# Stick-breaking attention with TensorE's order written out, the next pair's projections woven in, and products moved to GpSimd

## The chip, the cores and the metric

One core of a Trainium2 chip runs the whole program. The metric is device time in microseconds: 2575.24 us before (median of three runs, 2574.47 to 2579.44). Engines are named as the profile names them: PE is TensorE (PEld its weight loads), DVE is VectorE, ACT is ScalarE, POOL is GpSimd, SP issues the DMAs.

## The reference

A trunk of two layers over 1,024 rows of 1,024 features. Each layer is a token mixer and a SwiGLU. Layer 0 mixes with sliding-window attention (16 query heads, 2 key heads, window 128, softmax with sinks), layer 1 with stick-breaking attention (16 heads of 64). What the change touches most is the latter:

```
z = einsum('bqhd,bshd->bhqs', qb, k) * scale          # qb: 128 queries of one block
log_beta = log_sigmoid(z)
log_one_minus = where(strict, log_sigmoid(-z), 0.0)   # strict: key index < query index
rc = cumsum(log_one_minus, axis=3, reverse=True)
after = pad(rc[..., 1:], one column of zeros at the end)
a = where(strict, exp(log_beta + after), 0.0)
o = einsum('bhqs,bshd->bqhd', a, v)
```

In words: the weight of a key is sigmoid(z) times the product of sigmoid(-z) over all later keys before the query.

## The kernel before, in words

Every f32 matrix product runs on rounded halves: a value is split into a high part (an ACT cast to fp32r) and a low part (value minus high, a DVE or POOL subtraction), and three products stand for one (`mm3`, L100: high x high, high x low, low x high).

**The stages** on the trace's clock: norms and conditioning to about 120 us; sliding-window attention to about 345 us (`stage1` to `stage3`, L473 to L556); its output projection with the next norm (`out_proj`, L626) to about 480 us; SwiGLU to about 1165 us (`gates`, `down`); stick-breaking attention to about 1780 us (L965 to L1141); then out_proj and SwiGLU of layer 1 with the same functions.

**Stick-breaking** goes by pairs of heads, p = 0 to 7. `proj_pair(p)` (L1020) makes Q, K and the low part of K (`kl`) for two heads, and V: 3 weights x 2 halves of the rows x 8 blocks of the features x 3 products = 144 matmuls of 512 columns into banks `psd`. Each head's Q holds its high part in 64 partitions and its low part in the other 64, so that K and `kl` are needed in both halves of the partitions: L1037 to L1044 make the doubles with four more ACT casts per half.

Then 8 steps per pair, one for each head `par` and each block `c` of 256 queries. `attn_a` (L1067) takes two tiles of 128 queries, i = 2c and 2c+1, with L = 128(i+1) keys: score matmuls into `psz` (two, and a mask), two sigmoids on ACT (L1084 `nb` with the sign turned, L1085 `bb`), a reversed running product of `nb` on DVE in place (L1089, the scan; its two inputs `nb` and `ones` both lie in SBUF), and the product `bb` x `nb` on DVE (L1091, both inputs in SBUF too). `attn_v` (L1095) takes the finished tiles 256 keys at a time: four transposes into `pst` (L1103), the high part `ah` on ACT (L1106), the low part `al` on DVE (L1107; it reads `pst` in PSUM and `ah` in SBUF), four matmuls with V into `psa`. V's two halves of 64 columns give the high and low results in two halves of the partitions: `tm` (L1114) copies one half, `ob` (L1115) adds, and a DMA stores 64 rows. The steps come in the order c = 0, 3, 1, 2 for each head, `attn_v` one step behind `attn_a` (`lag`, L1122). `proj_pair(p+1)` is emitted behind the eight steps of pair p.

**What sets the order:** the program is emitted as above, and a scheduler of the framework orders each engine's instructions by emission, readiness and its own costs; each engine then runs its list strictly in order. So the projections of the next pair do stand between the steps of this one, where the scheduler put them. Pair 7 has no projections beside it; it loads and splits the output weights instead (`load_o`, L353, eight times: a DVE product L356, an ACT cast L298, a DVE split L299).

**Output projection** (`out_proj`, `block`, L632): a block of 128 rows loads the stored attention result, ACT casts it, POOL subtracts (L636, in `split_into` L299), PE multiplies. Sliding-window attention stores its result as stick-breaking does (L552 to L556: `tm`, `ob` with one buffer, 64 rows).

Of the kernel before, what the change touches and what calls it, by code (L numbers as in the profile page):

```python
# [18 lines left out]
P = 128  # L19
# [45 lines left out]
def build(tc, x_in, c_in, pos_in, ada_w, ada_b, n1g, n2g, wqkv_a, qn_a, kn_a, sinks, wo_a,  # L65
# [30 lines left out]

    def mm(o, l, r, start, stop, more=False):
        nc.tensor.matmul(o, l, r, start=start, stop=stop, skip_group_check=more)  # L98
# [6 lines left out]
    def tr(o, i, n=P):  # L105
        nc.tensor.transpose(o, i, ident[:n, :n])  # L106
# [280 lines left out]
    odA = [dr.tile([HD, 16, P], F32, name=f"odA{b}") for b in range(NB)]  # L387
# [41 lines left out]
    def keys_values(b):  # L429
# [20 lines left out]
        for j in range(4):  # L450
            nc.tensor.transpose(pt[:, j * P : (j + 1) * P], kdf[:, j], identr)
# [37 lines left out]
    def stage2(g, b, qs, r):  # L489
        QT = wk.tile([P, 8, P], F32R, tag="QT", name=nm("QT"), bufs=2)  # L490
        qsf = qs.rearrange("p h e d -> p h (e d)")
        for j in range(2):
            pt = bank("t", F32R)
            for h in range(4):
                nc.tensor.transpose(pt[:, h * P : (h + 1) * P], qsf[:, 4 * j + h], identr)
            nc.scalar.copy(QT[:, 4 * j : 4 * j + 4], pt.rearrange("p (h t) -> p h t", t=P))
# [34 lines left out]
    def stage3(g, b, sm):  # L531
        for j in range(2):
# [93 lines left out]
    def out_proj(p, W, od, x_src, l, gi, first):  # L626
# [338 lines left out]
    def nt_tile(shape, dt):  # L965
        return nbp.tile(shape, dt, tag="nt", name=nm("nt"), bufs=3)

    def load_b(p, j):
        raw = ad.tile([P, KT, P], F32, tag="ad", name=nm("wr"), bufs=2)
        nc.sync.dma_start(raw, wB[:, j * D + p * P : j * D + (p + 1) * P].rearrange("(k p) n -> p k n", p=P))  # L970
        t = wqp.tile([P, 2, KT, P], F32R, tag="whl", name=nm("whl"), bufs=4)
        return split_into(t[:, 0], t[:, 1], raw, scale=0.125 if j == 0 else None)
# [33 lines left out]
    odB = [dr.tile([HD, 16, 256], F32, name=f"odB{c}") for c in range(4)]  # L1006

    def proj_t(p, j):
        wh, wl = w0[j] if p == 0 else load_b(p, j)
        for half in range(2):  # L1010
            th, tl = HB[half]
            if p == 0 and half == 0 and j in first_b:
                pb = first_b[j]
            else:
                pb = bank("d")
                for k in range(KT):
                    mm3(pb, wh[:, k], wl[:, k], th[:, k], tl[:, k], k == 0, k == KT - 1)
            yield half, pb

    def proj_pair(p):  # L1020
# [4 lines left out]
        V = wb.tile([P, NB, 2, P], F32R, tag="V", name=nm("V"), bufs=1)  # L1025
        A, B = slice(0, HD), slice(HD, P)

        def q_(half, pb):
            s = slice(half * 512, half * 512 + 512)
            nc.scalar.copy(Q[0][A, s], pb[A])  # L1030
            nc.scalar.copy(Q[1][B, s], pb[B])
            sub(Q[0][B, s], pb[A], Q[0][A, s])
            sub(Q[1][A, s], pb[B], Q[1][B, s])

        def k_(half, pb):
            s = slice(half * 512, half * 512 + 512)
            nc.scalar.copy(K[0][A, s], pb[A])  # L1037
            nc.scalar.copy(K[1][B, s], pb[B])
            nc.scalar.copy(K[0][B, s], pb[A])
            nc.scalar.copy(K[1][A, s], pb[B])  # L1040
            sub(kl[0][A, s], pb[A], K[0][A, s])
            sub(kl[1][B, s], pb[B], K[1][B, s])
            nc.scalar.copy(kl[0][B, s], kl[0][A, s].bitcast(F32))
            nc.scalar.copy(kl[1][A, s], kl[1][B, s].bitcast(F32))  # L1044

        if p == 0:
            q_(0, first_b[0])
            k_(0, first_b[1])
        for half, pb in proj_t(p, 0):
            if p or half:  # L1050
                q_(half, pb)
        for half, pb in proj_t(p, 1):
            if p or half:
                k_(half, pb)
        for half, pb in proj_t(p, 2):
            vt = nt_tile([P, 512], F32)
            nc.scalar.copy(vt, pb)
            pt = bank("t")
            for b in range(4):
                tr(pt[:, b * P : (b + 1) * P], vt[:, b * P : (b + 1) * P])  # L1060
            v4 = pt.rearrange("p (b u d) -> p b u d", u=2, d=HD)
            o = V[:, half * 4 : half * 4 + 4]
            nc.scalar.copy(o[:, :, :, 0:HD], v4)
            sub(o[:, :, :, HD:P], v4, o[:, :, :, 0:HD])
        return Q, K, kl, V

    def attn_a(p, par, c, Q, K, kl, V):  # L1067
        bs = []
        for i in (2 * c, 2 * c + 1):
            L = P * (i + 1)  # L1070
            n = max(256, L if L <= 512 else L // 2)
            nb = wb.tile([P, S], F32, tag="nb", name=nm("nb"), bufs=2)
            bb = wb.tile([P, S], F32, tag="bb", name=nm("bb"), bufs=4)
            tq = slice(i * P, i * P + P)
            for s0 in range(0, L, n):
# [46 lines left out]
    def step(p, par, c, cur, lag):  # L1122
        pend.append(attn_a(p, par, c, *cur))
        while len(pend) > lag:
            attn_v(*pend.pop(0))
# [55 lines left out]
```

## Time and profile before

| | us |
|---|---|
| median of three runs | 2575.24 |
| the profiled execution, its own time | 2575.87 |
| its span, first to last instruction | 2574.1 |
| PE busy in the span | 2392.6 (93%) |
| DVE busy | 1679.6 (65%) |
| ACT busy | 1069.7 (42%) |
| POOL busy | 478.4 (19%) |

The mean granted clock of PE is 0.968 of full. Busy shares are means over stages with different limits, and a busy PE is not a PE at its peak, since a matmul's end is modelled and overlaps the next one: a matmul of 512 columns is shown with 390 ns and more, and follows the one before by 227 ns where PE is not held up. So a stage is judged by what its matmuls would take at their undisturbed spacing, against the time that it takes.

### The profile page before, as it was taken

How to read it: one execution, taken by the hardware profiler on the slowest of the kernel's cores; microseconds unless marked ns; L12 is line 12 of the kernel's file. 1: busy time of each engine (PE TensorE's matmuls, PEld its weight loads, DVE VectorE, ACT ScalarE, POOL GpSimd, SP SyncE). 2: the span in 40 equal slices, each digit the busy share in tenths (PEclk: the TensorE clock that was granted, in tenths of full speed). 3: DMA queues.
4: the chain of work that ended last, by engine and by line, in shares of the span. 5: the costliest groups of instructions: out<-in, count | busy, mean ns of one | idle time of the engine just before them, and what ended most of it. 6: DMA issues, size and time to landing. Idle time of an engine off the chain costs nothing.

```text
span 2574.1 us, 31259 instructions
## 1 busy us (share of the span) xinstructions
PE 2392.6 (93%) x11404; PEld 1937.7 (75%) x11404; DVE 1679.6 (65%) x2509; ACT 1069.7 (42%) x2077; POOL 478.4 (19%) x545
## 2 busy tenths in 40 slices
PE   6898788899999999999999999997989999999999
PEld 5776667678787878887777777776768888887887
DVE  7689854765767667436888777777365544557553
ACT  4487633423232232115666666664343333333110
POOL 2344533122232300001000000002213223220000
PEclk9799889899999999999999999998989999999999
DMA  8113266233535364202101111013412222226311
GB/s 280 49 42 93 82 173 201 66 110 125 175 122 180 106 229 143 71 25 83 40 26 28 28 33 32 24 41 96 140 53 91 91 66 90 92 80 236 104 50 66
DMA packets 159033, 248.59 MB, mean 97 GB/s; under 512 B 10256, under 2 KB 109728, under 8 KB 158880
## 3 DMA queue, kind: packets, MB, share of 16 engines
q1 hardware_dynamic: 158256, 246.46, 30.2%
q8 instruction: 90, 1.47, 0.2%
q14 instruction: 63, 0.52, 0.1%
q10 hardware_dynamic: 624, 0.14, 0.0%
HBM read 198.33 MB, written 48.23 MB: 96 GB/s over the span
## 4 chain that ended last, share of the span: by engine, by line
PE 67%; DVE 15%; ACT 5%; DMA 5%; issue 4%; POOL 3%; SPq 0%; ACTq 0%; DVEq 0%; POOLq 0%
PE psz L98 23%; PE psd L98 20%; PE pst L98 17%; PE psa L98 6%; DVE nb L1089 4%; DMA ada<-in_ada_w_dram 3%; DVE bb L1091 2%; DVE al L109 1%; DVE acc L258 1%; ACT sm L525 1%; PE pst L106 1%; POOL rg L299 1%; ACT ah L1106 1%; DVE sl L623 1%; DVE ob L1115 1%
## 5 line engine op out<-in xcount | busy, mean ns | idle before, releaser
L622 ACT CAST sh<-rg 128x512 fp32r<-128x512 f32 x308 | 191.5, 622 | 563.6 <-PE psz L98 252.4
L623 DVE TENSOR_TENSOR sl<-rg,sh 128x512 fp32r<-128x512 f32 x308 | 236.5, 768 | 79.5 <-ACT sh L622 79.5
L98 PE MATMUL psd<-hth,whl 128*128 128x512 f32 x768 | 255.8, 399 | 0.6 <-DVE QK L109 0.6
L298 ACT CAST dh<-raw 128x1024 fp32r<-128x1024 f32 x88 | 87.8, 1049 | 279.3 <-PE psa L98 176.1
L1089 DVE TENSOR_TENSOR_SCAN nb<-nb,ones 128x128 f32<-128x128 f32 (+7 forms) x128 | 170.4, 1343 | 29.7 <-ACT nb L1084 28.7
L98 PE MATMUL psd<-htl,whl 128*128 128x512 f32 x384 | 156.5, 408 | 2.2 <-DVE htl L109 2.2
L98 PEld LDWEIGHTS psd<-hth,whl 128*128 128x128 f32 x768 | 141.3, 189 | 22.2 <-DVE QK L109 1.1
L98 PE MATMUL psz<-hT,sh 128*128 128x512 f32 x352 | 140.7, 402 | 10.8 <-DVE f L800 6.3
L98 PE MATMUL psz<-lT,sh 128*128 128x512 f32 x352 | 140.2, 398 | 2.4 <-DVE lT L109 2.4
L790 POOL TENSOR_TENSOR rg<-rg,rg 128x512 f32<-128x512 f32 x44 | 59.1, 1343 | 441.2 <-DMA rg<-in_w_up_dram 316.7
L98 PE MATMUL psz<-hT,sl 128*128 128x512 f32 x352 | 139.4, 396 | 0.0
L98 PE MATMUL psd<-hB,sh 128*128 128x512 f32 x352 | 137.2, 390 | 0.0
L98 PE MATMUL psd<-hB,sl 128*128 128x512 f32 x352 | 137.0, 389 | 0.0
L98 PE MATMUL psd<-lB,sh 128*128 128x512 f32 x352 | 137.0, 389 | 0.0
L258 DVE SCALAR_TENSOR_TENSOR acc<-ada,condT,acc 128x1024 f32<-128x1024 f32 x77 | 117.9, 1531 | 27.9 <-DMA ada<-in_ada_w_dram 26.6
L1087 POOL MEMSET bb<- 128x128 f32 x64 | 13.2, 206 | 561.9 <-PE pst L106 436.6
L109 DVE TENSOR_TENSOR al<-pst,ah 128x512 fp32r<-128x512 f32 x160 | 104.1, 678 | 19.2 <-ACT ah L1106 18.7
L98 PE MATMUL psz<-QK,QK 128*128 128x384 f32 (+4 forms) x384 | 111.6, 378 | 4.0 <-ACT bb L1085 3.9
L98 PE MATMUL psa<-ah,V 128*128 128x256 f32 x320 | 94.5, 305 | 21.5 <-DVE ob L1115 14.2
L1084 ACT ACTIVATE nb<-psz 128x320 f32<-128x320 f32 (+4 forms) x192 | 93.3, 505 | 43.4 <-DVE bb L1091 35.8
L299 DVE TENSOR_TENSOR dl<-raw,dh 128x1024 fp32r<-128x1024 f32 x88 | 104.6, 1218 | 8.8 <-ACT dh L298 8.8
L98 PE MATMUL psa<-al,V 128*128 128x256 f32 x320 | 93.8, 316 | 16.3 <-DVE al L109 15.4
(329 smaller groups left out, 6491.9 us busy)
## 6 DMA issues: line engine op xcount, KB each, us to landing
ada<-in_ada_w_dram SPq DMA_DIRECT2D x96, 512.0 KB, 5.1
rg<-in_w_gate_dram SPq DMA_DIRECT2D x44, 512.0 KB, 3.6
rg<-in_w_up_dram SPq DMA_DIRECT2D x44, 512.0 KB, 6.3
raw<-hid SPq DMA_DIRECT2D x44, 512.0 KB, 6.8
raw<-in_w_down_dram SPq DMA_DIRECT2D x44, 512.0 KB, 4.5
hid<-f SPq DMA_DIRECT2D x64, 256.0 KB, 2.1
wr<-in_wqkv_b_dram SPq DMA_DIRECT2D x24, 512.0 KB, 3.9
xsp<-xt SPq DMA_DIRECT2D x16, 512.0 KB, 4.3
```

Of the source, the lines that this page charges most:

```text
L98: nc.tensor.matmul(o, l, r, start=start, stop=stop, skip_group_check=more)
L106: nc.tensor.transpose(o, i, ident[:n, :n])
L109: return nc.vector.tensor_tensor(o, a, h.bitcast(F32), op=ALU.subtract)
L258: i = nc.vector.scalar_tensor_tensor(a, wt, condT[:, j : j + 1], a, op0=ALU.mult, op1=ALU.add)
L298: nc.scalar.copy(h, raw)
L299: (eng or nc.vector).tensor_tensor(l, raw, h.bitcast(F32), op=ALU.subtract)
L622: nc.scalar.copy(hv, src)
L623: nc.vector.tensor_tensor(lv, src, hv.bitcast(F32), op=ALU.subtract)
L790: nc.gpsimd.tensor_tensor(A[1, 0], A[1, 0], A[1, 1], op=ALU.add)
L1084: nc.scalar.activation(nb[:, s0 : s0 + e], pz[:, 0:e], AF.Sigmoid, scale=-1.0)
L1089: nc.vector.tensor_tensor_scan(rv, rv, ones[:, 0:1].to_broadcast([P, L]), initial=1.0, op0=ALU.mult, op1=ALU.mult)
L1091: nc.vector.tensor_tensor(bb[:, 0 : L - 1], bb[:, 0 : L - 1], nb[:, 1:L], op=ALU.mult)
```

## The change

- **Order.** Inside pairs 0 to 6 every PE instruction is tied to the one emitted before it, so PE's order there is the emitted one. The emission is a weave: `scores` (was `attn_a`), `values` (was `attn_v`) and `proj_gen` (was `proj_pair`) are generators that stop at marked places, and `weave` takes them in turn by the share that is done. A step now has the scores of its own tiles, the values of the step two before (`LAG` = 2), and 6 or 7 of the 50 pieces of the next pair's projections (a piece: three matmuls of 512 columns). The steps' order is c = 3, 2, 0, 1. Pair 7 is not tied.
- **Moved to POOL:** the product `bb` x `nb` (16 tiles per pair), and the low parts of the next pair's K and V weights (two of three; Q's, which carries the scale, stays on DVE).
- **DMA:** the doubles of K and `kl` are copied from SBUF to SBUF by DMA on SP, eight per pair.
- **Result:** both attentions now store both halves (128 rows, one ACT copy, no DVE add; twice the bytes), and `out_proj` loads the high and the low rows as two tensors (four DMAs for two, twice the bytes), casts on ACT, and makes the low part with a subtraction and an addition on DVE instead of one subtraction on POOL.
- **Buffers:** `nb` 3 (2), `bb` 6 (4), V one tile per head in 3 (one tile for both in 1), `nt` 2 (3), `whl` 3 (4), the sliding window's `ob` 2 (1).

```diff
+    def chained(i):
+        if pe["on"] and pe["prev"] is not None:
+            tc.add_manual_dep(i.ins, pe["prev"].name, ..., reason="order")
+        pe["prev"] = i.ins if pe["on"] else None
     def mm(o, l, r, start, stop, more=False):
-        nc.tensor.matmul(o, l, r, start=start, stop=stop, skip_group_check=more)
+        chained(nc.tensor.matmul(o, l, r, start=start, stop=stop, skip_group_check=more))
...
-            tm = wk.tile([HD, 512], F32, tag="tm", name=nm("tm"), bufs=1)
-            ob = wk.tile([HD, 512], F32, tag="ob", name=nm("ob"), bufs=1)
-            nc.scalar.copy(tm, av[HD:P])
-            nc.vector.tensor_tensor(ob, av[0:HD], tm, op=ALU.add)
+            ob = wk.tile([P, 512], F32, tag="ob", name=nm("ob"), bufs=2)
+            nc.scalar.copy(ob, av)
...
-            raw = ring(p, [P, KT, P])
-            for par in range(2):
-                nc.sync.dma_start(raw[par * HD : (par + 1) * HD], od(b, par))
-            oh, ol = split_into(ring(p, [P, KT, P], F32R), ring(p, [P, KT, P], F32R), raw, eng=nc.gpsimd)
+            raw, ol = ring(p, [P, KT, P]), ring(p, [P, KT, P], F32R)
+            low = ol.bitcast(F32)
+            for e, t in enumerate((raw, low)):
+                for par in range(2):
+                    nc.sync.dma_start(t[par * HD : (par + 1) * HD], od(b, par)[e * HD : (e + 1) * HD])
+            oh = ring(p, [P, KT, P], F32R)
+            nc.scalar.copy(oh, raw)
+            nc.vector.tensor_tensor(raw, raw, oh.bitcast(F32), op=ALU.subtract)
+            nc.vector.tensor_tensor(ol, raw, low, op=ALU.add)
...
+    def same(o, i):
+        nc.sync.dma_start(o.bitcast(F32), i.bitcast(F32))
+    def proj_gen(p):
...
+        w = w0 if p == 0 else [load_b(p, j, nc.gpsimd) for j in range(3)]
+        yield Q, K, kl, V
...
+                    for k in range(KT):
+                        mm3(pb, wh[:, k], wl[:, k], th[:, k], tl[:, k], k == 0, k == KT - 1)
+                        yield
...
+                    nc.scalar.copy(K[0][A, s], pb[A])
+                    nc.scalar.copy(K[1][B, s], pb[B])
+                    same(K[0][B, s], K[0][A, s])
+                    same(K[1][A, s], K[1][B, s])
...
-            nc.vector.tensor_tensor(bb[:, 0 : L - 1], bb[:, 0 : L - 1], nb[:, 1:L], op=ALU.mult)
+            nc.gpsimd.tensor_tensor(bb[:, 0 : L - 1], bb[:, 0 : L - 1], nb[:, 1:L], op=ALU.mult)
...
+        turn(0)                                   # transposes, ah, al of 256 keys
+        yield
+        for u in range(c + 1):
+            if u < c:
+                turn(u + 1)
+                yield
+            prod(u)                               # four matmuls with V
+            if u < c:
+                yield
+        ob = wb.tile([P, 256], F32, tag="ob", name=nm("ob"), bufs=2)
+        nc.scalar.copy(ob, o)
...
+    def weave(parts):
+        todo = sorted(((i + 0.5) / n, j) for j, (_, n) in enumerate(parts) for i in range(n))
+        for _, j in todo:
+            next(parts[j][0], None)
...
+            gen = proj_gen(p + 1)
+            nxt = next(gen)
+            for n, (par, c) in enumerate((par, c) for par in range(2) for c in (3, 2, 0, 1)):
+                parts = [(scores(p, par, c, *cur), STOPS[c])]
+                if len(ready) >= LAG:
+                    v = ready.pop(0)
+                    parts.append((values(*v), 2 * v[2] + 2))
+                parts.append((gen, (7, 6, 6, 6)[n % 4]))
+                weave(parts)
```

PE in the middle of a pair, before (`psd` is a projection, `psz` scores, `pst` transposes, `psa` the product with V):

```order
L98 MATMUL psa_1921_10312<-al_1924_10319,V_1824_9850 128x256
L98 MATMUL psa_1921_10312<-ah_1923_10318,V_1824_9850 128x256
L98 MATMUL psa_1921_10312<-al_1924_10319,V_1824_9850 128x256
L106 MATMUL pst_1937_10366<-ident_69,bb_1914_10282 128x128
L106 MATMUL pst_1937_10366<-ident_69,bb_1918_10298 128x128
L106 MATMUL pst_1937_10366<-ident_69,bb_1914_10282 128x128
L106 MATMUL pst_1937_10366<-ident_69,bb_1918_10298 128x128
L98 MATMUL psz_1954_10428<-QK_1822_9848,QK_1821_9847 128x384
L98 MATMUL psz_1954_10428<-QK_1823_9849,QK_1821_9847 128x384
L98 MATMUL psd_1990_10593<-hth0_1758_9576,whl_1989_10590 128x512
L98 MATMUL psa_1933_10352<-ah_1935_10358,V_1824_9850 128x256
L98 MATMUL psd_1990_10593<-htl0_1759_9577,whl_1989_10590 128x512
```

PE in the second step of pair 2 in the change (c = 2 with the values of c = 1), from the last transpose of the second 256 keys to the product of the first:

```order
L116 MATMUL pst_2140_11486<-ident_69,bb_2100_11324 128x128
L108 MATMUL psd_2138_11473<-hth1_1728_9538,whl_2112_11366 128x512
L108 MATMUL psd_2138_11473<-htl1_1729_9539,whl_2112_11366 128x512
L108 MATMUL psd_2138_11473<-hth1_1728_9538,whl_2112_11366 128x512 x2
L108 MATMUL psd_2138_11473<-htl1_1729_9539,whl_2112_11366 128x512
L108 MATMUL psd_2138_11473<-hth1_1728_9538,whl_2112_11366 128x512
L108 MATMUL psz_2145_11503<-QK_1950_10640,QK_1949_10639 128x384
L108 MATMUL psz_2145_11503<-QK_1951_10641,QK_1949_10639 128x384
L108 MATMUL psa_2134_11459<-ah_2136_11465,V_1889_10364 128x256
L108 MATMUL psa_2134_11459<-al_2137_11466,V_1889_10364 128x256
L108 MATMUL psa_2134_11459<-ah_2136_11465,V_1889_10364 128x256
L108 MATMUL psa_2134_11459<-al_2137_11466,V_1889_10364 128x256
```

Before, the scheduler's order had single projections between the pieces of one product. Now they come in groups of three, each product with V whole, one or two groups and some scores behind its transposes.

DVE at the heaviest tiles of a pair, before (the list names the scan of L1089 SCALAR_TENSOR_TENSOR):

```order
L1089 SCALAR_TENSOR_TENSOR nb_2332_12213<-nb_2332_12213,ones_78 128x896
L1091 TENSOR_TENSOR bb_2333_12214<-bb_2333_12214,nb_2332_12213 128x895
L1089 SCALAR_TENSOR_TENSOR nb_2336_12229<-nb_2336_12229,ones_78 128x1024
L109 TENSOR_TENSOR al_2343_12251<-pst_2341_12245,ah_2342_12250 128x512
L1091 TENSOR_TENSOR bb_2337_12230<-bb_2337_12230,nb_2336_12229 128x1023
L1115 TENSOR_TENSOR ob_2345_12259<-psa_2340_12244,tm_2344_12258 64x256
L1089 SCALAR_TENSOR_TENSOR nb_2346_12263<-nb_2346_12263,ones_78 128x384
```

DVE in the first two steps of pair 2 in the change:

```order
L119 TENSOR_TENSOR al_2124_11400<-pst_2122_11394,ah_2123_11399 128x512
L1101 SCALAR_TENSOR_TENSOR nb_2118_11383<-nb_2118_11383,ones_78 128x896
L1101 SCALAR_TENSOR_TENSOR nb_2126_11418<-nb_2126_11418,ones_78 128x1024
L119 TENSOR_TENSOR al_2137_11466<-pst_2135_11460,ah_2136_11465 128x512
L119 TENSOR_TENSOR QK_2105_11358<-psd_2117_11379,QK_2105_11358 64x512
L119 TENSOR_TENSOR QK_2108_11361<-psd_2117_11379,QK_2108_11361 64x512
L1101 SCALAR_TENSOR_TENSOR nb_2131_11452<-nb_2131_11452,ones_78 128x640
L119 TENSOR_TENSOR al_2142_11492<-pst_2140_11486,ah_2141_11491 128x512
```

The products and the `ob` additions are gone from DVE's list; scans and low parts alternate, and `al` of the second 256 keys stands behind the 640-column scan.

POOL, which had only a memset (206 ns) per step in this stage before, in the same steps of the change:

```order
L309 TENSOR_TENSOR whl_2116_11376<-wr_2115_11374,whl_2116_11376 128x1024
L1099 MEMSET bb_2132_11453 128x128
L1103 TENSOR_TENSOR bb_2119_11384<-bb_2119_11384,nb_2118_11383 128x895
L1103 TENSOR_TENSOR bb_2127_11419<-bb_2127_11419,nb_2126_11418 128x1023
L1099 MEMSET bb_2156_11556 128x128
L1103 TENSOR_TENSOR bb_2132_11453<-bb_2132_11453,nb_2131_11452 128x639
L1103 TENSOR_TENSOR bb_2144_11502<-bb_2144_11502,nb_2143_11501 128x767
```

The products stand in the order of the tiles, the weight splits between them.

## Rows read from the trace of the kernel before

**Rows 1.** Busy by stretch: start:end, length, busy us of each engine, granted clock, DMA share, GB/s.
```profile
240.00:345.00 105.00, 73.67 (x344) 57.07 (x343) 93.02 (x203) 66.88 (x187) 51.97 (x56) 0.81 0.34 102
345.00:410.00 65.00, 56.51 (x250) 46.29 (x249) 31.97 (x27) 14.75 (x21) 24.93 (x17) 0.87 0.80 233
1216.00:1722.00 506.00, 474.87 (x2655) 373.25 (x2653) 401.58 (x515) 335.25 (x701) 11.51 (x56) 1.00 0.11 30
1722.00:1780.00 58.00, 39.49 (x184) 29.53 (x183) 54.71 (x63) 35.58 (x74) 5.69 (x7) 0.79 0.29 71
```
**Rows 2.** Chain of work that ended last, 1216 to 1722 us: shares, then start us, us, what.
```profile
by line: PE psd L98 28.3%; DVE nb L1089 17.3%; issue 10.9%; PE psa L98 9.9%; DVE bb L1091 6.5%; DVE al L109 5.7%; PE pst L106 3.2%; ACT ah L1106 3.0%; DVE ob L1115 2.6%; DVE QK L109 1.8%; ACT nb L1084 1.7%; PE psz L98 1.6%; ACT bb L1085 1.5
...
1346.51 10.68 PE psd L98 x47
1418.27 10.67 PE psd L98 x47
```
**Rows 3.** Timeline of PE: start us, us, what; matmuls that follow without a wait.
```profile
1314.22 0.27 PE L98 MATMUL psa<-al,V 128*128 128x256 f32 x1
...
1314.92 0.28 PE L98 MATMUL psa<-al,V 128*128 128x256 f32 x1
1315.04 1.04 PE L106 MATMUL pst<-ident,bb 128*128 128x128 f32 x8
```
**Rows 4.** Waits, 1216 to 1722 us: who waited for whom, us in total, times, longest.
```profile
PEld psa L98 <- DVE al L109: 24.5, 46, 1.0
PEld psa L98 <- ACT ah L1106: 22.8, 50, 1.0
```
**Rows 5.** Groups of DVE and ACT, 1216 to 1722 us: count, busy, mean ns, idle before.
```profile
L1089 DVE TENSOR_TENSOR_SCAN nb<-nb,ones 128x128 f32<-128x128 f32 (+3 forms) x113 | 149.3, 1335 | 29.7 <-ACT nb L1084 28.7
L109 DVE TENSOR_TENSOR al<-pst,ah 128x512 fp32r<-128x512 f32 x140 | 90.8, 679 | 13.7 <-ACT ah L1106 13.1
L1091 DVE TENSOR_TENSOR bb<-bb,nb 128x127 f32<-128x127 f32 (+3 forms) x113 | 82.4, 739 | 2.4
...
L1115 DVE TENSOR_TENSOR ob<-psa,tm 64x256 f32<-64x256 f32 x56 | 22.7, 406 | 10.5 <-ACT tm L1114 10.1
L299 DVE TENSOR_TENSOR whl<-wr,whl 128x1024 fp32r<-128x1024 f32 x12 | 14.6, 1216 | 0.2
...
L1084 ACT ACTIVATE nb<-psz 128x128 f32<-128x128 f32 (+3 forms) x170 | 82.2, 503 | 36.6 <-DVE bb L1091 29.4 <-PE psz L98 5.8
...
L1106 ACT CAST ah<-pst 128x512 fp32r<-128x512 f32 x140 | 78.1, 596 | 23.5 <-PE pst L106 21.8 <-ACT QK L1031 0.7
```
**Rows 6.** Group of POOL over the span: out_proj's split of 1,024 columns.
```profile
L299 POOL TENSOR_TENSOR rg<-rg,rg 128x1024 fp32r<-128x1024 f32 x16 | 41.9, 2622 | 66.8 <-ACT rg L298 66.8
```
**Rows 7.** Timeline, 1769.5 to 1776 us: POOL and DVE side by side.
```profile
1770.21 4.46 POOL L299 TENSOR_TENSOR rg<-rg,rg 128x1024 fp32r<-128x1024 f32 x1 [7.30 <-ACT rg L298]
1770.25 2.27 DVE L1089 TENSOR_TENSOR_SCAN nb<-nb,ones 128x1024 f32<-128x1024 f32 x1
1772.45 0.66 DVE L109 TENSOR_TENSOR al<-pst,ah 128x512 fp32r<-128x512 f32 x1
1773.04 2.71 DVE L1091 TENSOR_TENSOR bb<-bb,nb 128x1023 f32<-128x1023 f32 x1
```
**Rows 8.** Group of DVE, 120 to 360 us: the sliding window's addition.
```profile
L555 DVE TENSOR_TENSOR ob<-psa,tm 64x512 f32<-64x512 f32 x32 | 21.7, 677 | 8.8 <-ACT tm L554 8.3 <-DMA odA<-ob 0.4
```
**Rows 9.** Chain, 240 to 345 us: one piece.
```profile
339.52 3.96 DMA odA<-ob
```
**Rows 10.** Chain, 375 to 402 us: one block of the output projection, of three alike.
```profile
377.69 4.79 DMA rg<-odA
382.58 1.06 ACT rg L298
383.76 2.69 POOL rg L299
```
**Rows 11.** Group of DVE, 1722 to 1780 us (pair 7).
```profile
L1091 DVE TENSOR_TENSOR bb<-bb,nb 128x127 f32<-128x127 f32 (+7 forms) x16 | 13.4, 837 | 0.1
```

More of the change, by code (lines that the diff above doesn't have):

```diff
@@ L386, in build @@
     cm_kt, kt = pools.open("ktA", "left")
-    odA = [dr.tile([HD, 16, P], F32, name=f"odA{b}") for b in range(NB)]
+    odA = [dr.tile([P, 16, P], F32, name=f"odA{b}") for b in range(NB)]
     def hA_blk(b, k):
@@ L1005, in build @@
     cm_wb, wb = pools.open("wkB", "left")
[L1006 to L1020, printed above, removed]
+    odB = [dr.tile([P, 16, 256], F32, name=f"odB{c}") for c in range(4)]
+    A, B = slice(0, HD), slice(HD, P)
+    def same(o, i):
+        nc.sync.dma_start(o.bitcast(F32), i.bitcast(F32))
+    def proj_gen(p):
         Q, K, kl = [], [], []
@@ L1024, in proj_pair @@
                 t.append(xq.tile([P, S], F32R, tag="xq", name=nm("QK"), bufs=NQ))
[L1025 to L1064, printed above, removed]
@@ L1068, in attn_a, with scores @@
+    def scores(p, par, c, Q, K, kl, V):
         bs = []
@@ L1107, in attn_v, with prod, drain @@
             sub(al_, pt, ah_)
+            a[u] = ah_, al_
+        def prod(u):
+            ah_, al_ = a[u]
             for e in range(2):
                 sb = 2 * u + e
-                mm(o, V[:, sb, par], ah_[:, e * 256 : (e + 1) * 256], u == 0 and e == 0, False)
-                mm(o, V[:, sb, par], al_[:, e * 256 : (e + 1) * 256], False, u == c and e == 1)
-        tm = wb.tile([HD, 256], F32, tag="tm", name=nm("tm"), bufs=2)
-        ob = wb.tile([HD, 256], F32, tag="ob", name=nm("ob"), bufs=2)
-        nc.scalar.copy(tm, o[HD:P])
-        nc.vector.tensor_tensor(ob, o[0:HD], tm, op=ALU.add)
-        nc.sync.dma_start(odB[c][:, 2 * p + par], ob)
-    nxt = proj_pair(0)
-    row_b = grow_make(1, 0)
-    pend = []
[L1122 to L1125, printed above, removed]
+                mm(o, V[par][:, sb], ah_[:, e * 256 : (e + 1) * 256], u == 0 and e == 0, False)
+                mm(o, V[par][:, sb], al_[:, e * 256 : (e + 1) * 256], False, u == c and e == 1)
+        turn(0)
+        yield
+        for u in range(c + 1):
+            if u < c:
+                turn(u + 1)
+                yield
+            prod(u)
+            if u < c:
+                yield
+        ob = wb.tile([P, 256], F32, tag="ob", name=nm("ob"), bufs=2)
+        nc.scalar.copy(ob, o)
+        nc.sync.dma_start(odB[c][:, 2 * p + par], ob)
+        yield
+    ready = []
+    LAG = 2
+    def weave(parts):
+        todo = sorted(((i + 0.5) / n, j) for j, (_, n) in enumerate(parts) for i in range(n))
+        for _, j in todo:
+            next(parts[j][0], None)
+    def drain(g):
+        for _ in g:
+            pass
+    gen = proj_gen(0)
+    nxt = next(gen)
+    drain(gen)
+    row_b = grow_make(1, 0)
+    STOPS = {0: 2, 1: 2, 2: 4, 3: 4}
     W = []
@@ L1130, in build @@
         if p < 7:
-            for n, (par, c) in enumerate([(0, 0), (0, 3), (0, 1), (0, 2), (1, 0), (1, 3), (1, 1), (1, 2)]):
-                step(p, par, c, cur, 1 if n < 7 else 0)
+            pe["on"], pe["prev"] = True, None
             if p == 6:
@@ L1139, in build @@
             for n, (c, par) in enumerate((c, par) for c in range(4) for par in range(2)):
-                step(p, par, c, cur, 1 if n < 7 else 0)
+                drain(scores(p, par, c, *cur))
+                while len(ready) > (1 if n < 7 else 0):
+                    drain(values(*ready.pop(0)))
                 load_o(W, wo_b[0], n, row_b, ad, "ad")
```

71 lines of the change are left out of this document (56 added, 15 removed).

## The prediction

> **What bounds the kernel now.** I read the busy table by stretch first: four stretches are touched. In stick-breaking, pairs 0 to 6 (1216 to 1722 us), PE is busy 475 of 506 us and DVE 402; in pair 7 DVE 54.7 of 58; at the end of the sliding window DVE 93 of 105 with PE at a granted clock of 0.81; in the first output projection the DMA share is 0.80 [rows 1]. Then the chain of waits of the first stretch: PE has under half of it, and the scans, products, `al` and `ob` of DVE together about 32% [rows 2]. The chain shows why: each pair has one undisturbed run of 47 projections (10.68 us, so 0.227 us for a matmul of 512 columns), seven such runs in all, and they come every 71.76 us [rows 2]. That is the tail of the next pair's projections, when DVE has little to do; in the rest of the pair PE waits in small pieces for `al` and `ah` [rows 4].
>
> How much of a pair PE needs: 144 projections x 0.227 = 32.7 us. The 80 products with V follow at (1314.92 - 1314.22)/6 = 0.117 us, 9.3 us; the 88 transposes at (1.04 - 0.27)/7 = 0.11 us, 9.7 us [rows 3]. The scores are 18,944 columns at 0.227/512 us, 8.4 us, and 16 masks at, by estimate, 0.05 us, 0.8 us. Sum 60.9 us of 71.8: a pair loses 10.9 us, seven pairs 76 us. That is the most that order and cover can give.
>
> **The change in pairs 0 to 6.** DVE had 401.6/506 x 71.76 = 57.0 us per pair. It loses the products (82.4/506 x 71.76 = 11.7), the additions `ob` (3.2) and two weight splits of 1.2, and keeps 39.7 [rows 5]. ACT had 47.6 and loses eight casts of K and `kl` (some 4.8 at the 0.6 us of a 512-column cast) [rows 1, 5]. The doubles by DMA are ready a third of a pair before they are read, so I cost them at nothing; SP's list has room (DMA share 0.11) [rows 1]. POOL gets 9,200 columns of products (2 x (128 x 36 - 8)) and two splits of 1,024. Its split of 1,024 columns takes 2.62 us on average [rows 6], so 23.5 + 5.2 = 28.7 us.
>
> All of that fits beside 60.9 us of PE, but DVE and POOL don't run freely side by side. At 1770 us a POOL split and a scan started together: the split took 4.46 us instead of 2.6, the scan its usual 2.27; `al` then ran in 0.66 us beside the split; the product behind it took 2.71 us and ended 1 us after the split, so it had waited for it [rows 7]. So a scan and a POOL instruction that reads SBUF exclude each other, while `al`, with one input in PSUM, does not mind. Scans (21.2 us per pair), Q's weight split (1.2) and POOL's reads (28.7) make 51 us that can't overlap in a pair of 60.9.
>
> I walked the two heaviest steps (c = 3, then c = 2) with these durations, t = 0 at the pair's first projection. The 896-column scan ends at 6.7, its product holds POOL from 6.8 to 9.1. The 1,024-column scan, ready at 8.2, waits for it and ends at 11.3; its product runs 11.4 to 14.0. The 640-column scan, ready at 13.2, waits until 14.0 and ends at 15.5. Behind it in DVE's list stands `al` of the second 256 keys, whose transposes were done at 10.9: it ends at 16.1, and PE wants it at 14.2. PE stands 1.8 us. Nothing else can run there, since PE's order is fixed. Later in the half a weight cast on ACT (some 1.05 us, twice `ah`'s columns) delays `ah` for another 0.4 us. The second half has the same, 2.2 us; there POOL's weight split stands between two products and delays the next scan, about 0.8 us more; and V's transposes come two matmul groups behind the copy that they need, about 1 us. Sum 6.2 us per pair. The first transposes of c = 3 come at 15.3, 1.3 us behind their product: no wait, but little room.
>
> Without the exclusion the same place gives 0.7 us instead of 1.8, and the pair 4 us.
>
> The Trainium skill, SBUF — State Buffer, section Who interferes with whom, states it as a rule: a VectorE instruction with two SBUF inputs contends with a GpSimd instruction that reads SBUF, and the loser waits for the whole instruction. The rule speaks against moving the products beside the scans; the trace agrees, with 4.46 and 2.71 us [rows 7]. By the rule the pair stands 6.2 us, without it 4.
>
> So a pair takes 60.9 + 6.2 = 67.1 instead of 71.8 us: 4.7 x 7 = 33 us gained. Ends: 76 gained with no stall at all; 20 gained if DVE stops for the whole of each POOL read (39.7 + 28.7 = 68.4, and 0.5 for what PE adds); a loss if PE's fixed order adds to that, which is the slower rival.
>
> **The other places.** *Sliding window:* 32 additions of 0.68 us leave DVE, 21.7 us in all [rows 8], in a stage that DVE binds at its end only [rows 1]; and the one chain piece of 3.96 us in which `ob`'s single buffer waits for its store goes with the second buffer [rows 9]. ACT's copy costs the same for 128 rows as `tm` did for 64, since both have 512 columns. Between 0 and 21.7; I take 7 gained: the 4 us and a few of the additions. Next late there are softmax's other DVE work and ACT.
>
> *Output projection, twice:* per block POOL's split of 2.6 us goes and two DVE instructions of 1.2 us come, the same 2.4; the load doubles. The chain shows a block as load 4.8, cast 1.06, split 2.7 [rows 10]. The low rows can land during cast and subtraction. 4 MB more at the 233 GB/s of that stretch are 17 us of DMA [rows 1], which PE hides but for the three blocks that the chain already waits for: 0 to 12, I take 4 lost. In layer 1 there are no conditioning loads beside it: 1 lost.
>
> *Pair 7:* no projections cover anything. DVE loses 13.4 us of products [rows 11] and 2.4 of additions, but a tile's product takes 2.6 us instead of 1.2 and excludes scans and `load_o`'s products and splits. Scans 21, `load_o`'s and products on POOL 23 make about 55 in series, against 54.7 of DVE [rows 1]: -3 to +10, I take 4 lost. *Norm ahead of pair 0:* `nt` 2 buffers for 3, 1 lost.
>
> Sum: -33 - 7 + 4 + 1 + 4 + 1 = -30 us. The profiled execution took 2575.9 us, its span 2574.1, the median 2575.2, so nothing has to be converted: 2545 us.
>
> **Rivals.**
>
> *The weave covers nearly everything.* For it: `al` has two or three groups of projections as cover, 2 us or more, and DVE falls from 57 to 40 us. Against: the first two steps of a half have eight sigmoids each, the longest ones, so at the mean of 0.5 us, with two `ah` of 0.6 and the copies out of PSUM, ACT has by estimate some 6 us of work or more in a step of 7.5 [rows 5]. With 2 us of stalls a pair is 62.9: 8.9 x 7 = 62 gained, with the other terms -62 - 7 + 4 + 1 + 4 + 1 = -59, 2516 us.
>
> *DVE and POOL in series set the pace.* 68.4 us of DVE and POOL in series, 69 with PE's share: 20 gained, pair 7 at its upper end (10 lost), the window 7: 2575 - 20 - 7 + 4 + 1 + 10 + 1 = 2564 us. For it: the 51 us that can't overlap, and that products follow their scans at once, so that the next scan usually meets one. Against: `al`, Q and K work runs beside POOL.
>
> *Slower: PE's fixed order makes every late product a stop of PE.* Place: the first transposes of a step, which wait for POOL's product of two steps before (room 1.3 us in the walk), and `al`, which waits behind scans. A stop there delays the scores that feed ACT, the scans and the next products, so the pair runs in a ring of scan, product, transpose: 68.4 us in series and the 6 to 8 us of stalls on top, 75 to 76 us per pair, 30 lost, with the other terms 2575 + 30 - 7 + 10 = 2608 us. It decides from a stall of 10.9 us per pair, 1.4 per step. Before, the scheduler's order could put projections into such a gap [rows 2].
>
> *The stage's gain is eaten elsewhere:* the forecast's 33 with DMA at 12 lost, pair 7 at 10 lost and no gain in the window: 2566 us; it lies in the second rival's range.
>
> **How the numbers follow.** Forecast 50% (2528 to 2556), good cover 22% (2500 to 2528), in series or eaten 15% (2556 to 2576), slower 13% (2576 to 2615). The range that holds 8 of 10: 2508 to 2580. Differences under 0.2%, 5 us, can't be told from none. Faster: 50 + 22 and 9 of the 15, 0.81; same: the other 6, 0.06; slower 0.13.
>
> **What would show it.** Right: the undisturbed runs of 47 projections vanish; the pairs' period, read from Q's casts, is 65 to 69 us; POOL is busy some 30 us per pair; scans that meet a product are longer by up to 2.6 us (mean above 1.33), products by up to 2.3; PE's waits in the stage name `al` behind a scan. Wrong in the gaining sense: a period under 64. Wrong in the losing sense: a period over 70, with the transposes waiting for POOL's products by more than 1 us at a time; or an output projection longer by more than 12 us, waiting for its loads.

## The result

| | median, us | runs | ratio to before (95%) |
|---|---|---|---|
| before | 2576.61 | 4 (2574.47 to 2579.44) | |
| the change | 2511.26 | 4 (2506.01 to 2518.0) | 0.9746 (0.9732 to 0.9761) |

The change is 65 us faster; forecast were 30. The time lies just inside the range (2508 to 2580); the gain is more than twice the forecast. The profiled execution of the change took 2506.01 us (span 2504.3), 69.9 less than that of before, and is the fastest of its four.

Where the profiled time went, by points that both traces have (the first matmul or store of a stage):

| place | before | after | difference | forecast |
|---|---|---|---|---|
| start to the first matmul of out_proj, layer 0 | 346.2 | 324.2 | -22.0 | -7 |
| to SwiGLU's first store | 153.5 | 151.2 | -2.3 | +4 |
| to the first transpose of the norm ahead of pair 0 | 669.0 | 667.5 | -1.5 | 0 |
| to the last projection (norm, pairs 0 to 6) | 551.5 | 508.6 | -42.9 | -32 |
| to the last product with V (pair 7) | 69.4 | 64.9 | -4.5 | +4 |
| to the last matmul of out_proj, layer 1 | 92.1 | 98.6 | +6.5 | +1 |
| to the end | 692.4 | 689.3 | -3.1 | 0 |

Of the 40 us that these two executions gained more than forecast, the sliding window has 15, the pairs have 11 and pair 7 has 8.5. A steady pair lost 7.4 us instead of 4.7, which would make 19 in seven pairs; pair 6, which is not steady, gave a part back. The second row's gain is a lucky execution: in the change and twelve kernels below that share its program up to stick-breaking, the stretch took 151.2 to 158.6 us, 155.8 in the middle, so out_proj costs some 2 us, near the forecast 4.

### The profile page after: what moved, and what is told of

It reads as the page before. It is cut to its first block, busy times and chain, and to the rows that moved or that the text cites. A ratio compares the mean times of both kernels' runs of the same rounds, so it can differ in the third digit from the quotient of the medians.

```text
span 2504.3 us, 31440 instructions
## 1 busy us (share of the span) xinstructions
PE 2359.5 (94%) x11404; PEld 1934.1 (77%) x11404; DVE 1604.8 (64%) x2319; ACT 1036.6 (41%) x2029; POOL 646.4 (26%) x671
## 4 chain that ended last, share of the span: by engine, by line
PE 70%; DVE 9%; DMA 4%; issue 2%; ACT 2%; POOL 1%; SPq 0%; DVEq 0%; ACTq 0%; POOLq 0%
PE psz L108 24%; PE psd L108 21%; PE pst L108 16%; PE psa L108 5%; DMA ada<-in_ada_w_dram 2%; PE pst L116 2%; DVE nb L1101 2%; DVE acc L268 1%; DVE al L119 1%; DVE lT L119 1%; DVE Wl L309 0%; DMA wr<-in_wo_b_dram 0%; DVE QK L119 0%; DVE sl L631 0%; ACT nb L1094 0%
## 5 line engine op out<-in xcount | busy, mean ns | idle before, releaser
L631 DVE TENSOR_TENSOR sl<-rg,sh 128x512 fp32r<-128x512 f32 x308 | 244.8, 795 | 94.0 <-ACT sh L630 94.0
L108 PE MATMUL psd<-hth,whl 128*128 128x512 f32 x768 | 304.3, 415 | 0.1
L1103 POOL TENSOR_TENSOR bb<-bb,nb 128x895 f32<-128x895 f32 (+7 forms) x128 | 179.1, 1402 | 248.7 <-DVE nb L1101 159.5
L1101 DVE TENSOR_TENSOR_SCAN nb<-nb,ones 128x896 f32<-128x896 f32 (+7 forms) x128 | 192.4, 1508 | 44.3 <-ACT nb L1094 41.9
L108 PEld LDWEIGHTS psd<-hth,whl 128*128 128x128 f32 x768 | 146.5, 191 | 22.2 <-issue 1.3
L268 DVE SCALAR_TENSOR_TENSOR acc<-ada,condT,acc 128x1024 f32<-128x1024 f32 x77 | 111.0, 1441 | 25.5 <-DMA ada<-in_ada_w_dram 24.8
L1094 ACT ACTIVATE nb<-psz 128x448 f32<-128x448 f32 (+3 forms) x192 | 95.3, 496 | 65.6 <-PE psz L108 61.3
L1124 ACT CAST ah<-pst 128x512 fp32r<-128x512 f32 x160 | 94.2, 591 | 54.1 <-PE pst L116 51.8
L108 PE MATMUL psz<-QK,QK 128*128 128x384 f32 (+4 forms) x384 | 104.7, 356 | 2.5 <-ACT bb L1095 2.4
```

The costliest lines, as they stand in the source:

```text
L108: chained(nc.tensor.matmul(o, l, r, start=start, stop=stop, skip_group_check=more))
L268: i = nc.vector.scalar_tensor_tensor(a, wt, condT[:, j : j + 1], a, op0=ALU.mult, op1=ALU.add)
L631: nc.vector.tensor_tensor(lv, src, hv.bitcast(F32), op=ALU.subtract)
L1094: nc.scalar.activation(nb[:, s0 : s0 + e], pz[:, 0:e], AF.Sigmoid, scale=-1.0)
L1101: nc.vector.tensor_tensor_scan(rv, rv, ones[:, 0:1].to_broadcast([P, L]), initial=1.0, op0=ALU.mult, op1=ALU.mult)
L1103: nc.gpsimd.tensor_tensor(bb[:, 0 : L - 1], bb[:, 0 : L - 1], nb[:, 1:L], op=ALU.mult)
```

## The profile after

Busy by stretch, as in [rows 1] (start:end, length, engines, granted clock, DMA share, GB/s). The sliding window now ends at 324 us, so the first row stops there and the second, as long as that of before, holds 21 us of the output projection. The steady stage is 1216 to 1652 us, pair 7 the last row:

```profile
240.00:324.00 84.00, 69.32 (x352) 53.84 (x351) 79.22 (x177) 65.24 (x198) 42.86 (x54) 0.90 0.42 130
240.00:345.00 105.00, 90.26 (x445) 70.46 (x445) 90.02 (x189) 70.20 (x206) 46.91 (x60) 0.92 0.52 156
345.00:410.00 65.00, 60.51 (x288) 49.84 (x287) 37.91 (x45) 22.16 (x34) 10.77 (x14) 1.00 0.97 249
1216.00:1652.00 436.00, 427.29 (x2500) 356.93 (x2499) 304.19 (x333) 291.82 (x619) 186.16 (x171) 0.99 0.21 58
1652.00:1717.00 65.00, 49.64 (x276) 40.63 (x276) 62.03 (x57) 42.22 (x91) 30.33 (x24) 0.87 0.38 93
```

PE fills 98% of the stage where it filled 94. In the last part of the sliding window PE is busy 69 of 84 us, at a mean granted clock of 0.90 of the full 2.4 GHz; before, it was busy 74 of 105 us at 0.81 [rows 1]. The next two lines are one cast of Q in two neighbouring pairs, from ACT's timeline: the period is 64.36 us (four in a row 64.34 to 64.37; before, five from 71.74 to 71.78).

```profile
1395.34 0.58 ACT L1050 CAST QK<-psd 64x512 fp32r<-64x512 f32 x1 [0.36 <-PE psd L108]
...
1459.70 0.58 ACT L1050 CAST QK<-psd 64x512 fp32r<-64x512 f32 x1 [0.36 <-PE psd L108]
```

PE's waits between these two casts (who waited for whom: us, times, longest), and one of them in PE's timeline:

```profile
PEld psa L108 <- DVE al L119: 1.0, 2, 0.7
PE psa L108 <- DVE al L119: 0.5, 1, 0.5
PEld pst L116 <- ACT nt L1065: 0.3, 1, 0.3
PEld pst L116 <- DVE al L119: 0.2, 1, 0.2
```

```profile
1401.51 0.39 PE L108 MATMUL psa<-al,V 128*128 128x256 f32 x1 [0.48 <-DVE al L119]
```

The wait is the one that the walk named (`al` of the second 256 keys), but 0.5 us long, not 1.8. Most of what this pair takes beyond the 60.9 us counted for PE is no wait with a name: from start to start its 144 projections take 35.5 us, where 32.7 were counted. The groups of DVE and POOL, 1258 to 1588 us, five pairs, as in [rows 5, 6]:

```profile
L1101 DVE TENSOR_TENSOR_SCAN nb<-nb,ones 128x896 f32<-128x896 f32 (+3 forms) x80 | 118.4, 1480 | 33.4 <-ACT nb L1094 31.2 <-POOL bb L1103 2.0
L119 DVE TENSOR_TENSOR al<-pst,ah 128x512 fp32r<-128x512 f32 x100 | 68.2, 686 | 46.0 <-ACT ah L1124 43.8
...
L1103 POOL TENSOR_TENSOR bb<-bb,nb 128x511 f32<-128x511 f32 (+3 forms) x81 | 109.1, 1349 | 161.2 <-DVE nb L1101 99.9 <-ACT ob L1145 33.6 <-ACT ah L1124 16.2
L309 POOL TENSOR_TENSOR whl<-wr,whl 128x1024 fp32r<-128x1024 f32 x11 | 32.2, 2929 | 0.0
```

A scan takes 1480 ns on average instead of 1335 [rows 5], 2.3 us per pair more, and a weight split 2929 instead of 2400 alone: the exclusion is there. `al` is unchanged. POOL's timeline and then DVE's show which side pays:

```profile
1429.70 2.00 POOL L1103 TENSOR_TENSOR bb<-bb,nb 128x1023 f32<-128x1023 f32 x1 [2.29 <-PE psz L108]
1431.67 3.57 POOL L309 TENSOR_TENSOR whl<-wr,whl 128x1024 fp32r<-128x1024 f32 x1
1435.19 2.77 POOL L1103 TENSOR_TENSOR bb<-bb,nb 128x639 f32<-128x639 f32 x1
```

```profile
1427.14 2.42 DVE L1101 TENSOR_TENSOR_SCAN nb<-nb,ones 128x1024 f32<-128x1024 f32 x1 [1.64 <-ACT nb L1094]
...
1431.51 1.55 DVE L1101 TENSOR_TENSOR_SCAN nb<-nb,ones 128x640 f32<-128x640 f32 x1
1432.97 0.66 DVE L119 TENSOR_TENSOR al<-pst,ah 128x512 fp32r<-128x512 f32 x1
1434.03 2.81 DVE L1101 TENSOR_TENSOR_SCAN nb<-nb,ones 128x768 f32<-128x768 f32 x1 [0.40 <-ACT nb L1094]
```

The 1,023-column product takes 2.00 us where I had priced 2.6. It ends 0.2 us after the 640-column scan starts, and this scan is hardly longer for it (1.55 us, alone 1.49); the split that starts 0.16 us behind the scan waits (3.57). The 768-column scan waits for the split (2.81 for 1.75), but PE's list above has no wait longer than 0.3 us behind it.

## The experiments

Periods are those of the steady pairs in each profile; times are medians, each ratio against runs of the kernel before on the same chip. Where a difference is under 10 us the time of one kernel alone scatters too much (2506 to 2518 for the change), and the period decides.

**Stick-breaking: order, room, offloads.** Only the products, moved to POOL in the kernel before:

```
-            nc.vector.tensor_tensor(bb[:, 0 : L - 1], ..., nb[:, 1:L], op=ALU.mult)
+            nc.gpsimd.tensor_tensor(bb[:, 0 : L - 1], ..., nb[:, 1:L], op=ALU.mult)
```

> The kernel before with only the products moved to POOL. Theory 'offload': DVE falls from 57 to 45 us per pair and the period from 71.8 to 66 to 68 us, time 2535 to 2550. Rival 'order': the scheduler's order of PE keeps its waits, the period stays at 70 to 73 us, time 2565 to 2585.

2615.84 us, ratio 1.0143 (1.0117 to 1.0168), period 77 to 78: slower by 40 us, which neither side expected. PE's list has one step in hand there, and its transposes wait for POOL's product; here in 130 us (1340 to 1470), in total, times and longest:

```profile
PEld pst L106 <- POOL bb L1091: 10.4, 7, 3.5
PE pst L106 <- POOL bb L1091: 8.4, 7, 3.2
```

The same with two steps in hand (`step(..., 2 if n < 7 else 0)`, six `bb`, three `whl`):

> The kernel before with the products on POOL, as in the run that moved only these (period 77 to 78 us), but with two steps in hand instead of one and six bb buffers. Theory 'room': its transposes waited for POOL's product up to 3.5 us at a time because the tile was asked for one step later; with two steps the period falls to 70 us or less. Rival 'order': the scheduler's own order of PE keeps it at 74 us or more.

2624.90 us, 1.0177 (1.0150 to 1.0204), period 78 to 80. The period is the second theory's, but its cause is not shown. In the middle of a pair two steps do take the transposes' wait away; the long one, up to 3.5 us, is left at the start of each pair. This kernel still empties its queue of finished steps at every pair's end (`else 0`), where the change carries two steps into the next pair, and it kept two `nb` buffers and the order 0, 3, 1, 2. The run shows that a lag of two is not enough, and not which of these is missing. The converse, the change with the products back on DVE (L1103 `nc.vector`):

> The change with the 16 products per pair back on DVE (L1103), nothing else undone. Theory 'order': the written order of PE has enough cover, whatever engine makes the products; DVE then has some 40 + 12 = 52 us per pair under a PE of 62, and the steady period stays at 64 to 65 us, the time within 5 us of 2511. Rival 'offload': DVE's relief is what gave the time; the scans and al queue behind products again, the period goes to 68 us or more and the time to 2535 or more.

2527.29 us, 0.9812 (0.9794 to 0.9829), period 67.4: between the two theories, 3.0 of the 7.4 us are the products'. With the weight splits on DVE and the doubles on ACT too:

> The change with products and weight splits back on DVE and the doubles of K back on ACT: of the edits in stick-breaking only the order, the lag of two and the buffers are left (and the result's two halves). With the products alone back on DVE the period was 67.4. Theory 'order': it stays at 67 to 69 us, so the order gives 3 to 5 of the 7.4 us and the offloads the rest; time 2527 to 2540. Rival 'all together': ACT, with 4.8 us of casts more per pair, and DVE now hold ah and al up, the period is 70 us or more, time 2550 or more.

2531.02 us, 0.9811 (0.9791 to 0.9831), period 68.4. So the order with its two steps and buffers gives 3.3 of the 7.4 us by itself, and the offloads 4.1 on top of it, though the products alone cost 6 without it. "The order" is several things here: the weave, the blocks' order 3, 2, 0, 1, steps carried from one pair into the next, and more buffers; of these the runs take apart only the number of steps. Is it the order or the room? First the change with `LAG = 1`, then the order-only kernel with `LAG = 1`:

> The change with LAG = 1: a step carries the values of the step just before it instead of two before. Theory 'room': with products on POOL a weight tile is done up to 4 us later than before, and with one step in hand the transposes wait for POOL's product, as they do where only the products were moved; the period goes from 64.4 to 68 us or more. Rival 'cover': the projections between scores and values hide this too; the period stays at 64.4 to 65.5.

> As the run with only the order (period 68.4), but with one step in hand instead of two. Theory 'room is needed for POOL's products only': with products on DVE, done 1.2 us behind their scan, one step in hand is enough, and the period stays at 68 to 71 us. Rival 'two steps are the order's whole worth': the transposes wait for DVE's products, the period is 75 us or more.

The first took 2659.74 us, 1.0312 (1.0282 to 1.0342), period 85.3; the second 2628.10 us, 1.0192 (1.0169 to 1.0216), period 81.8. PE's waits in the same 130 us of the first and of the second:

```profile
PEld pst L116 <- POOL bb L1103: 24.2, 10, 4.2
PE pst L116 <- POOL bb L1103: 21.2, 9, 3.9
```

```profile
PEld pst L116 <- DVE bb L1103: 20.1, 9, 3.4
PE pst L116 <- DVE bb L1103: 17.9, 8, 3.1
```

The written order with one step in hand is worse than the scheduler's, on either engine: the transposes come one step behind the scores, and scan and product don't fit into it. The same wait is absent with two. Next, the tie taken off (`pe["on"], pe["prev"] = False, None`):

> The change with PE's instructions not tied: the weave is still how the program is emitted, but the scheduler may reorder PE. If the tie matters, the scheduler pulls projections forward and they run out before the pair ends, the period is 66 us or more (time 2525 or more). If the emission alone does it, the period is 64 to 65 us and the time within 5 us of 2511.

2508.48 us, 0.9739 (0.9722 to 0.9756), period 64.36: the emission alone does it. PE's list in the two traces is the same up to 1640 us, late in pair 6, so the scheduler keeps the woven order where it isn't tied.

**The sliding window.** Buffers alone, in the kernel before (`tm` and `ob` halves of one 128-row tile with `bufs=2`); additions alone (`ob` a copy of the high rows, no `tm`, no addition); the part "Result" whole; the change with `bufs=1`:

> The kernel before; in the sliding window alone, tm and ob share a tile of 128 rows with two buffers, so that an addition no longer waits for the store before it. The additions stay on DVE. Theory 'additions': the stage is bound by DVE's list, and buffers give at most the one piece of 4 us in the chain; the first matmul of the output projection comes at 342 to 346 us. Rival 'buffer': the wait of the eviction holds PE's bank and lets the clock fall; it comes at 330 or earlier, against 346.2 before and 324.1 in the change.

> The kernel before with tm and the addition left out in the sliding window: ob is a copy of the high rows by ACT (the low rows of that stage's result are left out), with one buffer and the same 64-row store. Theory 'additions': without 32 additions of 0.68 us on DVE the first matmul of the output projection comes at 324 to 330 us instead of 346.2. Rival 'buffer': the single buffer still makes the eviction wait for its store; it comes at 338 or later.

> The kernel before with only the part 'Result' of the change: both attentions store both halves, the output projection loads high and low rows and splits on DVE. From the two traces: the window 22 us shorter, the first output projection 2 shorter, the second 5 to 7 longer, and in stick-breaking 3 us of DVE per pair less, of which the order that PE has before lets through 0 to 2 us per pair. Sum -18 to -32, so 2543 to 2558 us. If the window's gain came from anything else in the change, this kernel is within 8 us of 2576.

> The change with one buffer instead of two for the sliding window's ob, so an ACT copy waits for the store of the one before. Theory 'additions': the first matmul of the output projection stays within 4 us of 324.1. Rival 'buffer': it comes 8 us later or more.

The first matmul of out_proj (first time behind the durations), before, then buffers, then no additions, then the change:

```profile
L98 PE MATMUL psd<-Wh,rg x128: 387/389/797, 346.2 to 1857.1; 128*128 128x512 f32 x128
```

```profile
L98 PE MATMUL psd<-Wh,rg x128: 387/389/796, 346.9 to 1861.1; 128*128 128x512 f32 x128
```

```profile
L98 PE MATMUL psd<-Wh,rg x128: 387/389/796, 324.1 to 1833.9; 128*128 128x512 f32 x128
```

```profile
L108 PE MATMUL psd<-Wh,rg x128: 387/389/775, 324.2 to 1786.0; 128*128 128x512 f32 x128
```

The buffer gives nothing (2578.59 us, 1.0004, 0.9991 to 1.0017), the additions all of it (2550.92 us, 0.9903, 0.9883 to 0.9922). Two things go with an addition: its time in DVE's list, and the time for which it holds PE's bank `psa`, since it reads it. PE did wait for that before, here in 120 to 346 us:

```profile
PE psa L98 <- DVE ob L555: 9.9, 7, 2.7
```

No run takes these two apart. The part "Result" whole took 2555.04 us, 0.9909 (0.9887 to 0.9930), with 323.8 at this place and a period of 71.70, so the `ob` additions of stick-breaking gave 0.07 us per pair. With one buffer the change took 2514.52 us, 324.8 at this place.

**Price and exclusion.** The product as a subtraction (`op=ALU.subtract`):

> The change with the product on POOL replaced by a subtraction of the same tiles (the weights of the keys are then not those of the reference). The trace of the change shows a product of 1,023 columns in 2.00 us, and POOL's subtraction of 1,024 in 2.35 to 2.40. Theory 'price': my forecast was too slow because it priced the product like the subtraction; then the 1,023-column instruction takes 2.3 to 2.4 us, the steady period rises from 64.4 to 65.5 to 67 us, and the time to 2520 to 2530. Rival 'cover': the weave hides POOL at either price; the period stays within 0.4 us of 64.4 and the time within 5 us of 2511. Third: the price belongs not to the operation but to what runs beside it; then the instruction takes 2.00 us as before.

2509.74 us, period 64.34, 1,023 columns in 2.00 us: the third case, so this run did not test the price. Next, four forms of the product in each pair, among them `nb[:, 0 : L - 1]`, which isn't shifted against `bb`:

> The change with four forms of POOL's product in one pair (the weights are then not those of the reference): head 0, c = 3: the second operand not shifted by one column; head 1, c = 3: not shifted and one column more (1,024, 896); head 0, c = 2: the output written as fp32r; head 1, c = 2: as in the change. In the change 1,023 columns take 2.00 us and 767 take 1.55. Theory 'output type': only the fp32r form is dearer, 767 columns in some 1.8 us. Rival 'shift': the unshifted forms take 2.3 us for 1,023 columns. Third, 'even count': only the 1,024 and 896 columns are dearer, 2.35 and 2.05 us.

POOL's groups, 1260 to 1590 us: not shifted, not shifted with an even count, and the fp32r output:

```profile
L1104 POOL TENSOR_TENSOR bb<-bb,nb 128x1023 f32<-128x1023 f32 x5 | 12.1, 2413 | 11.5 <-PE pst L116 11.5
L1106 POOL TENSOR_TENSOR bb<-bb,nb 128x1024 f32<-128x1024 f32 x5 | 12.0, 2397 | 11.5 <-PE pst L116 11.5
...
L1108 POOL TENSOR_TENSOR bb<-bb,nb 128x767 fp32r<-128x767 f32 x5 | 7.7, 1546 | 8.8 <-ACT ah L1131 7.0 <-DVE nb L1101 1.8
```

It is the shift: 2.41 us without it, 2.00 with it. Output type and count play no part. This kernel's period is 65.6 (one run, 2523.72 us): with the dearer form on the c = 3 tiles alone a pair is 1.2 us longer. Now POOL's reads taken away (`nc.gpsimd.memset(bb[:, 0 : L - 1], 0.5)` for the product), and the weight splits back on DVE:

> The change with POOL's product replaced by a memset of the same tile, which reads nothing (the products are left out, the weights are not those of the reference). Theory 'covered': scans fall to their undisturbed lengths, but the period goes down by less than 0.7 us per pair from 64.4, so exclusion cost at most that much of PE. Rival (my walk): exclusion costs PE about 2 us per pair, the period falls to 62.5 us or less.

> The change with the low parts of the K and V weights split on DVE instead of POOL, two of 1.2 us per pair. Theory 'exclusion costs little here': the period stays within 0.4 us of 64.4. Rival (my prediction's walk): POOL's split between two products makes scans wait, 0.8 us per pair, and al with them; without it the period falls by 0.5 us or more.

In neither did the pair get shorter. The memset kernel: 2508.18 us, 0.9727 (0.9707 to 0.9748), but a period of 65.9 to 67.5, longer than with POOL's reads. The time is not longer than the change's even so, because pair 7 takes 55.5 us there and 64.9 in the change. POOL, DVE and PE in its second half of a pair:

```profile
1443.27 2.40 POOL L309 TENSOR_TENSOR whl<-wr,whl 128x1024 fp32r<-128x1024 f32 x1 [2.35 <-ACT whl L308]
```

```profile
1443.68 3.33 DVE L1101 TENSOR_TENSOR_SCAN nb<-nb,ones 128x640 f32<-128x640 f32 x1
1446.94 0.66 DVE L119 TENSOR_TENSOR al<-pst,ah 128x512 fp32r<-128x512 f32 x1
```

```profile
1447.65 0.39 PE L108 MATMUL psa<-al,V 128*128 128x256 f32 x1 [1.70 <-DVE al L119]
```

Without a product to wait for, the split starts 0.4 us ahead of the 640-column scan; the scan takes 3.33 us instead of 1.5, `al` is late, and PE stands 1.70 us. In the change the same two start the other way round, and POOL pays. The Trainium skill, SBUF — State Buffer, section Who interferes with whom, says that issue order decides who blocks; the two traces show it, 3.57 us for the split there, 3.33 for the scan here. In [rows 7], where the trace has the split only 0.04 us ahead, it was the split that paid. The memset does more than leave out reads: it doesn't wait for the scan either, so this run doesn't price the exclusion alone.

The split on DVE: 2508.05 us, 0.9724 (0.9696 to 0.9752), period 65.44, 1.1 longer: in a steady pair DVE's place is dearer than POOL's, against the walk's 0.8 us gained. Over the whole stage it is not, since pair 6 takes 65.9 us there and 69.8 in the change.

**The ends of the stage.** `load_o`'s product of layer 1 on POOL behind pair 6; V of pair 0 woven into pair 0; `load_o`'s low parts on POOL:

> The change with the output weights' product with their row (load_o, layer 1) on POOL and ordered behind the last product of pair 6. Theory 'pair 6 waits for load_o's loads': in pair 6 DVE's list has these products ahead of scans, and they wait for DMAs; without them pair 6 takes 64 to 66 us instead of 69.8, and pair 7, bound by DVE, loses some 10 us of DVE and is not longer; the time falls by 4 to 10 us from 2511. Rival: POOL's reads in pair 7 exclude its scans and POOL's list puts products behind loads, so pair 7 grows by what pair 6 gains: within 3 us of 2511, or slower.

> The change with the projections of V of pair 0 woven into pair 0 with those of pair 1, so that pair 0's scores start when its Q and K are there. Theory 'the head of the stage stands alone': scores start some 12 us earlier, pair 0 grows by the 17 pieces moved into it (12 us of PE), and what is gained is PE's idle time ahead of pair 0 and in it, 2 to 6 us. Rival: PE was busy there anyway; within 2 us.

> The change with load_o's last step (the low part of the output weights, 8 of 1.2 us, layer 1) on POOL. Theory 'DVE binds pair 7' (62 of 64 us): pairs 6 and 7 together get 4 to 8 us shorter and the time is 2503 to 2508. Rival 'exclusion': POOL's subtractions of 2.35 us meet the scans of pair 7, and the pair is not shorter; 2509 to 2520.

In the first, pair 6 falls from 69.8 to 64.4 us, so `load_o` is what holds it (in the change PE waits there for `al` once 3.6 us, behind a DVE product that waits for its load), but pair 7 grows from 64.9 to 80.6, since ACT's casts now wait for POOL (21.4 us): 2521.65 us, 0.9778 (0.9763 to 0.9793). In the second, scores start 38 us behind the norm's first transpose instead of 48, but the last projection comes at the same 508.5 us, as the rival said: 2513.84 us, 0.9758 (0.9737 to 0.9778). In the third, DVE in pair 7 falls from 62 to 56 us, POOL rises from 30 to 43, pair 7 takes 65.4: 2520.92 us, 0.9760 (0.9735 to 0.9785). In the last kernel 9 of the 14 us between the two profiled executions lie ahead of the stage. None of the three beats the change.

## Why the prediction was off

**The sliding window** is the step that failed most: "I take 7 gained: the 4 us and a few of the additions", with an end of 21.7. Measured is that end, 22. I read the chain's one wait for a store [rows 9] as the gain; without it nothing changed. DVE at 93 of 105 us and PE at a clock of 0.81 [rows 1] said that DVE's list bounds the stretch, and by that reading each DVE instruction in it counts in full. The additions' 21.7 us and the 22 gained agree with it; that PE's bank also comes free sooner without them is the reading that no run excludes.

**The pairs.** The place of the stall was right (`al` behind the 640-column scan), its size wrong: 1.8 us forecast in each half, 0.5 and less named in the trace. The failing step is "its product runs 11.4 to 14.0. The 640-column scan, ready at 13.2, waits until 14.0": priced by a POOL split, whose mean of 2.62 us held collisions (alone 2.35 to 2.40) and whose operands aren't shifted against each other. With 2.00 the scan hardly waits. The run above with the dearer form on four tiles of 16 puts 1.2 us per pair on that price, of 2.7 missed. By the walk's own lines `al` would then end near 15.3 and PE still stand some 1 us, so the walk was too slow elsewhere as well. The 0.8 us for the weight split is not among PE's waits, and the 1 us for V's transposes is 0.3. Against that, the projections took 2.8 us more than counted, without a wait that the profile names, so that 67.1 came as near to 64.4 as it did partly by luck. The exclusion itself, which I had also counted as PE's loss, falls mostly on POOL or on scans with room. How the rest divides is argued from these lines; no run took it apart.

**The slower rival** had the right mechanism and the wrong kernel: transposes that wait for a product make 82 to 85 us per pair with one step in hand. "No wait, but little room" for two steps held. The rival "weave covers nearly everything" came near the time (2516) by luck: it had 62.9 us per pair for 64.4 and a window of 7 for 22.

**Right:** POOL some 29 us per pair (149.5 of 330 us), scans above 1.33 us on average, the 47-projection runs gone. The period lies 0.6 us under the 65 to 69 expected. **Too dear or too cheap:** pair 7 gained 4.5 us where 4 lost were forecast; out_proj of layer 1 lost 6.5 for 1, where ACT waits 17.9 us for four loads of the stored rows (6.6 the longest); pair 6, which I took as steady, lost 5.4 to `load_o`.

## What to carry to other kernels

An offload and an order are worth little apart: products on POOL cost 40 us with the old order and gave 16 in the new one, because they lengthen a chain that a second step in hand keeps off PE, and the lag of two alone did not do it in the old emission. Where an engine's list is full in a stretch, price a change there by every instruction that leaves the list, not only by the waits that the chain shows. For two engines that exclude each other, don't add up their overlap: look which instruction starts first and what stands behind the loser.

## What the runs showed of the hardware

POOL's two-input instruction on f32 tiles is faster when the second operand starts one column further into its tile than the first: 1,023 columns in 2.00 us, 2.41 when both start alike. A product and a subtraction take the same when shifted (2.00), and the output as fp32r costs no more (767 columns in 1.55 us, as in f32). Other shifts, and why, were not tried.
